# Strassen products for the FFN up projection of a four-layer decoder trunk, with the FFN in two chunks

## The chip, the cores and the metric

The kernel runs on one core of one Trainium2 chip. The metric is the device time of one execution in microseconds (us). A core has five engines, each with a queue of its own that it works through in order: TensorE (PE in the profile; its weight loads are PEld), VectorE (DVE), ScalarE (ACT), GpSimd (POOL) and SyncE (SP), which here only issues transfers. Transfers between HBM and SBUF can be issued by SP, ACT and POOL.

## The reference, cut to what matters

One sequence of 512 tokens, width 1024, passes four blocks: a short-convolution mixer, a convolutional FFN, forgetting attention with 16 heads, and a second FFN.

```
xn = rmsnorm(x, g)
up = xn @ w_up                      # 1024 -> 2 x 2816
a, g = split(up, 2)
a = causal_dwconv(a, conv_w)        # 3 taps along the sequence
x = x + (silu(a) * g) @ w_down      # 2816 -> 1024
```

All inputs are float32. The kernel works feature-major: a tile is 128 features by 512 tokens.

## The kernel before, in words

Every float32 operand of a matrix product is split into a high part (rounded to the type fp32r by an ACT copy) and a low part (the remainder, a DVE subtraction). A product of two operands is three fp32r products: high by high, high by low, low by high. `mac` (lines 124 to 132) issues these three for each half of 256 tokens, so six matmuls for one 128x128 block of weights.

Weights come in tiles of 128 columns by up to 1024 elements. `weights` (line 114) issues the load on SP (line 119) into one of three raw buffers, and `parts` (lines 110, 111) splits it in pieces of 512. `gemm` (line 134) runs over the k tiles of one output tile; `gemm2` runs two output tiles together and holds back the last k tile of both, so that the newest input is asked for late.

The FFN (line 306) has 22 up tiles. For each, `gemm` makes `pa` (the convolved half) and `pg` (the gate), 8 k tiles each, hence 96 matmuls. DVE multiplies `pa` by the norm's `r` (line 316); `conv` is one ACT scaling (line 241) and two DVE instructions (lines 242, 244); ACT applies silu (line 192); DVE scales the gate (line 322), POOL multiplies (line 323), and ACT and DVE split the product (lines 162, 163). When all 22 results stand in SBUF, `project` (line 253) makes 8 output tiles with 22 k tiles each and adds them to the residual `x` (line 271). With `spill` it also writes the new `x` tile to a DRAM tensor `xsp` (line 277), and with `spilled` it reads the old one from there (line 250). Only the first FFN spills, and only the attention reads back.

The projection of the mixer (`a_out`) feeds the first FFN, that of the attention (`b_out`) the second. Their `norm.add` calls split each new `x` tile, scaled by the norm's gain, into the operands of the next products (lines 168, 169) and sum its square (lines 222, 224).

A scheduling layer builds each engine's queue from this program; it may move an instruction past others of its engine. What stands in a queue is issued in that order, and an instruction that waits holds back all that stands behind it.

## Time and profile before

| what | value |
|---|---|
| median of three runs | 1233.29 us (1231.23 to 1235.27) |
| the profiled execution | 1233.1 us, span in the trace 1231.3 us |
| PE busy / its weight loads | 1216.5 us (99%) / 1189.0 us |
| DVE / ACT / POOL busy | 678.6 us (55%) / 537.4 us (44%) / 203.1 us (16%) |
| HBM traffic | 100 GB/s over the span |
| granted TensorE clock, mean | 0.996 |

The page gives each engine's busy time and its share of the span. Matmuls overlap in the array, so a busy PE is read together with the distance between the starts of two matmuls. Other views list groups of equal instructions, single instructions in order of time (with the idle time before one and what ended it), stretches of time, and transfers.

### The profile page before, as it was taken

The page shows a single profiled execution, that of the slowest core. Times are in us where ns is not written, and L with a number is a line of the kernel's source. Part 1 is how long each engine was busy: PE and PEld are TensorE (multiplying, and loading weights), DVE is VectorE, ACT ScalarE, POOL GpSimd, SP SyncE. Part 2 cuts the span into 40 slices and gives each one's busy share as a digit, 9 for nine tenths or more (in the row PEclk, how much of TensorE's full clock was granted, in tenths as well). Part 3 has the DMA queues.
Part 4 walks back from the last instruction along what each step waited for, and adds up shares of the span by engine and source line. Part 5 has one row for each costly group of instructions (what it writes and reads, how often), then busy time and mean ns, then how long its engine had stood idle before and what let it go on. Part 6 is the DMA issues. An engine that isn't in the chain of part 4 may idle for free.

```text
span 1231.3 us, 24568 instructions
## 1 busy us (share of the span) xinstructions
PE 1216.5 (99%) x10425; PEld 1189.0 (97%) x10425; DVE 678.6 (55%) x1163; ACT 537.4 (44%) x973; POOL 203.1 (16%) x181
## 2 busy tenths in 40 slices
PE   9999999999999999999999899999999999999998
PEld 8999999999999999999998788889999999999998
DVE  6755556555555533344646787876565555553222
ACT  5433345334333433333556767775543334342221
POOL 0100021111111100000123435442111111110000
PEclk9999999999999999999999999999999999999999
DMA  6233233333333344342342212124233233233341
GB/s 215 87 103 101 88 104 92 97 104 93 97 104 91 93 130 125 121 140 87 95 139 79 84 52 86 53 87 129 86 104 101 89 103 101 89 99 104 116 119 45
DMA packets 39374, 124.14 MB, mean 101 GB/s; under 512 B 4384, under 2 KB 4896, under 8 KB 39264
## 3 DMA queue, kind: packets, MB, share of 16 engines
q1 hardware_dynamic: 38048, 120.41, 31.8%
q10 hardware_dynamic: 1152, 1.97, 0.5%
...
q0 software_dynamic: 64, 0.20, 0.0%
HBM read 118.33 MB, written 4.23 MB: 100 GB/s over the span
## 4 chain that ended last, share of the span: by engine, by line
PE 90%; ACT 4%; DVE 3%; POOL 2%; issue 1%; DMA 0%; SPq 0%; DVEq 0%; POOLq 0%; ACTq 0%
PE st L131 18%; PE st L130 17%; PE st L132 17%; PE mm L130 11%; PE mm L132 11%; PE mm L131 11%; ACT s L189 1%; PE st L620 1%; PE at L658 1%; PE st L649 1%; POOL m L667 1%; DVE s L624 1%; DVE wlo L111 1%; ACT g L189 1%; ACT g L162 1%
## 5 line engine op out<-in xcount | busy, mean ns | idle before, releaser
L130 PE MATMUL st<-g,whi 128*128 128x256 f32 x1686 | 465.5, 276 | 0.0
L131 PE MATMUL st<-g,whi 128*128 128x256 f32 x1686 | 465.4, 276 | 0.0
L132 PE MATMUL st<-g,wlo 128*128 128x256 f32 x1686 | 465.4, 276 | 0.0
L110 ACT CAST whi<-wraw 128x512 fp32r<-128x512 f32 (+1 forms) x394 | 240.4, 611 | 473.6 <-PE st L131 291.9
L111 DVE TENSOR_TENSOR wlo<-wraw,whi 128x512 fp32r<-128x512 f32 (+1 forms) x394 | 283.6, 720 | 222.9 <-ACT whi L110 218.3
L130 PE MATMUL mm<-g,whi 128*128 128x256 f32 x1242 | 346.2, 279 | 0.0
L131 PE MATMUL mm<-g,whi 128*128 128x256 f32 x1242 | 343.5, 277 | 0.0
L132 PE MATMUL mm<-g,wlo 128*128 128x256 f32 x1242 | 343.5, 277 | 0.0
L130 PEld LDWEIGHTS st<-g,whi 128*128 128x128 f32 x1686 | 316.6, 188 | 0.1
L131 PEld LDWEIGHTS st<-g,whi 128*128 128x128 f32 x1686 | 316.5, 188 | 0.1
L132 PEld LDWEIGHTS st<-g,wlo 128*128 128x128 f32 x1686 | 316.5, 188 | 0.0
L130 PEld LDWEIGHTS mm<-g,whi 128*128 128x128 f32 x1242 | 233.5, 188 | 1.8
L131 PEld LDWEIGHTS mm<-g,whi 128*128 128x128 f32 x1242 | 233.4, 188 | 1.3
L132 PEld LDWEIGHTS mm<-g,wlo 128*128 128x128 f32 x1242 | 233.2, 188 | 0.1
L323 POOL TENSOR_TENSOR m<-m,m 128x512 f32<-128x512 f32 x44 | 69.1, 1573 | 408.3 <-DVE m L322 370.9
L162 ACT CAST g<-m 128x512 fp32r<-128x512 f32 x66 | 40.8, 619 | 90.4 <-POOL m L323 66.8
L163 DVE TENSOR_TENSOR g<-m,g 128x512 fp32r<-128x512 f32 x51 | 36.8, 722 | 67.3 <-ACT g L162 66.7
L224 POOL TENSOR_TENSOR m<-m,m 128x512 f32<-128x512 f32 x21 | 27.9, 1330 | 175.5 <-ACT m L222 153.6
L640 POOL TENSOR_SCALAR s<-s,sm 128x128 f32<-128x128 f32 (+3 forms) x64 | 41.4, 660 | 75.5 <-DVE sm L637 69.2
L189 ACT ACTIVATE s<-s,bb 128x128 f32<-128x128 f32 (+3 forms) x64 | 35.4, 555 | 22.9 <-DVE bb L633 22.8
L241 ACT ACTIVATE m<-m,pr 128x512 f32<-128x512 f32 x52 | 37.7, 725 | 15.9 <-DVE m L316 13.0
L242 DVE SCALAR_TENSOR_TENSOR m<-m,pr,m 128x511 f32<-128x511 f32 x52 | 39.0, 750 | 9.5 <-ACT m L241 9.5
...
## 6 DMA issues: line engine op xcount, KB each, us to landing
wraw<-up SPq DMA_DIRECT2D x88, 512.0 KB, 3.5
...
wraw<-a_in SPq DMA_DIRECT2D x21, 512.0 KB, 3.6
wraw<-down SPq DMA_DIRECT2D x16, 512.0 KB, 3.5
wraw<-wqg SPq DMA_DIRECT2D x16, 512.0 KB, 3.6
wraw<-a_out SPq DMA_DIRECT2D x8, 512.0 KB, 3.5
ld<-xsp SPq DMA_DIRECT2D x16, 256.0 KB, 2.8
wraw<-wv SPq DMA_DIRECT2D x8, 512.0 KB, 3.6
```

Of the source, the lines that this page charges most:

```text
L110: nc.scalar.copy(out=hi[:, :n], in_=raw)
L111: nc.vector.tensor_tensor(out=lo[:, :n], in0=raw, in1=hi[:, :n].bitcast(F32), op=ALU.subtract)
L130: nc.tensor.matmul(ps[:, f], lhsT=lh[0], rhs=rh[0][:, f], start=go, stop=False, skip_group_check=True)
L131: nc.tensor.matmul(ps[:, f], lhsT=lh[0], rhs=rh[1][:, f], start=False, stop=False, skip_group_check=True)
L132: nc.tensor.matmul(ps[:, f], lhsT=lh[1], rhs=rh[0][:, f], start=False, stop=end, skip_group_check=True)
L162: nc.scalar.copy(out=hi, in_=src)
L163: (eng or nc.vector).tensor_tensor(out=lo, in0=src, in1=hi.bitcast(F32), op=ALU.subtract)
L189: chain["exp"] = ordered(nc.scalar.activation(**kw), chain["set"])
L241: nc.scalar.activation(out=y, in_=src, func=AF.Copy, scale=pr[:, col + 2:col + 3])
L242: nc.vector.scalar_tensor_tensor(out=y[:, 1:T], in0=src[:, 0:T - 1], scalar=pr[:, col + 1:col + 2], in1=y[:, 1:T], op0=ALU.mult, op1=ALU.add)
L323: nc.gpsimd.tensor_tensor(out=g, in0=g, in1=y, op=ALU.mult)
L640: nc.gpsimd.tensor_scalar(out=s, in0=s, scalar1=sm[:, e:e + 1], scalar2=1.0, op0=ALU.mult, op1=ALU.mult)
```

## The change

The up products of one tile are a product of a 2x2 block matrix of weights (convolved half and gate, by even and odd k tiles) with a 2x2 block matrix of inputs (even and odd k tiles, by the two halves of 256 tokens). Strassen's scheme makes them with seven block products for eight: 7 x 4 k pairs x 3 = 84 matmuls of 256 columns for 96. It needs sums and differences of the weight blocks, of the input blocks, and of the products.

- Weights: a new class `Up` loads two tiles of 1024 columns (`raw[0]`, `raw[1]`) on SP. `begin` adds HBM data onto `raw[1]` by an accumulating transfer that POOL issues (line 361), splits `raw[0]` (operands `cd`, lines 373 and 374), makes one difference on POOL (line 365), splits it (ACT line 368, POOL line 369), and then adds HBM data onto `raw[0]` by a second accumulating transfer (line 370). `end` splits both sums (`eb`, `fg`). Tile j+2 is loaded and tile j+1 begun while tile j is multiplied.
- Inputs: `NormS` makes the seven combinations for each pair of `x` tiles.
- Products: seven accumulations in three PSUM banks (lines 395 to 397); ACT copies three halves out (405, 406, 417); DVE combines them into one tile `ag` (lines 424 to 426). Both POOL multiplications (461, 462) follow silu.
- Chunks: after 11 up tiles `project` runs with 11 k tiles, then again after the other 11. So `x` is read from and written to `xsp` for each chunk, and the mixer's and the attention's projections spill each tile as well.
- Weight tiles of 1024 columns are split in one piece, and most pools are replaced by one pool of 18 tiles of 1024 columns (`wide`; names beginning with `w`).

```diff
-    def project(src, hs, nk, norm, last=False, spilled=False, spill=False, pss=()):
+    def project(src, hs, norm, last=False, spilled=False, spill=False, pss=(), k0=0, minus=False):
...
+                if minus:
+                    nc.vector.tensor_tensor(out=x[m][:, f], in0=old[:, f], in1=ps[:, f], op=ALU.subtract)
...
-        project(a_out, bu, KT, nxt)
+        project(a_out, bu, nxt, spill=True)
+
+    class Up:
+        def __init__(self, w):
+            self.raw = [W(), W()]
+            self.w = w
+            nc.sync.dma_start(out=self.raw[0], in_=w[:, 0:2 * T])
+            nc.sync.dma_start(out=self.raw[1], in_=w[:, 3 * T:5 * T])
+
+        def begin(self):
+            r0, r1 = self.raw
+            nc.gpsimd.dma_start(out=r1, in_=self.w[:, 0:2 * T], accum_op=ALU.add)
+            self.cd = W(F32R), W(F32R)
+            self.split(r0, self.cd)
+            a = M()
+            nc.gpsimd.tensor_tensor(out=a, in0=r0[:, 0:T], in1=r0[:, T:2 * T], op=ALU.subtract)
+            w = W(F32R)
+            self.a = w[:, 0:T], w[:, T:2 * T]
+            nc.scalar.copy(out=self.a[0], in_=a)
+            nc.gpsimd.tensor_tensor(out=self.a[1], in0=a, in1=self.a[0].bitcast(F32), op=ALU.subtract)
+            nc.gpsimd.dma_start(out=r0, in_=self.w[:, 2 * T:4 * T], accum_op=ALU.add)
...
+            ks = range(KT // 2)
+            for some in ((ks[:-1], ks[-1:]) if first else (ks,)):
+                for n in ("3", "4", "1", "5", "2") if first else ("3", "4"):
+                    for p in some:
+                        go(n, p)
+            self.s = M()
+            nc.scalar.copy(out=self.s[:, l], in_=b43[:, r])
+            nc.scalar.copy(out=self.s[:, r], in_=b43[:, l])
...
+            nc.vector.tensor_tensor(out=ag[:, HT:HT + T], in0=self.s, in1=self.b52, op=ALU.add)
+            nc.vector.tensor_tensor(out=two(t), in0=two(self.b43), in1=b1, op=ALU.add)
+            nc.vector.tensor_tensor(out=two(ag)[:, 0:4:3], in0=two(t), in1=two(self.b52), op=ALU.subtract)
...
         for j in range(JT):
+            pair = pairs.pop(j)
+            load(j + 2)
+            begin(j + 1)
+            pair.products(norm.xs, j == 0)
...
+            if j + 1 < JT:
+                pairs[j + 1].end()
+            ag = pair.results()
             a = M()
-            nc.vector.tensor_tensor(out=a, in0=pa, in1=r, op=ALU.mult)
+            nc.vector.tensor_tensor(out=a, in0=ag[:, 0:T], in1=r, op=ALU.mult)
             y = conv(a, col + 3 * j)
             act_silu(out=y, in_=y, func=AF.Silu)
...
+            nc.gpsimd.tensor_tensor(out=y, in0=y, in1=r, op=ALU.mult)
+            nc.gpsimd.tensor_tensor(out=y, in0=y, in1=ag[:, T:2 * T], op=ALU.mult)
+            us.append(split(y))
+            if j + 1 in cuts[1:]:
...
+                project(down, us, nxt if end else None, last and end, spilled=True, spill=spill or not end, k0=cuts[c - 1],
+                        minus=True)
+                us = []
```

In SP's queue at the end of the mixer's projection, before: eight loads of `a_out` weights follow each other (the last two are shown), and the loads of the first up tiles follow them.

```order
L119 DMA wraw_2146<-a_out 128x1024
L119 DMA wraw_2213<-a_out 128x1024
L119 DMA wraw_2280<-up 128x1024
L119 DMA wraw_2333<-up 128x1024
L119 DMA wraw_2429<-up 128x1024
```

In SP's queue in the mixer's projection of the changed program, from the first `a_out` load on (`xsp<-g` writes a finished `x` tile to DRAM, `ld<-xsp` reads one back):

```order
L122 DMA w_1654<-a_out 128x1024
L122 DMA w_1703<-a_out 128x1024
L320 DMA xsp<-g_83 128x512
L320 DMA xsp<-g_84 128x512
L122 DMA w_1796<-a_out 128x1024
L290 DMA ld_3889<-xsp 128x512
L290 DMA ld_3894<-xsp 128x512
L320 DMA xsp<-g_85 128x512
L122 DMA w_1858<-a_out 128x1024
L290 DMA ld_3978<-xsp 128x512
L320 DMA xsp<-g_86 128x512
L122 DMA w_1939<-a_out 128x1024
```

From the third output tile on, the load of a tile's weights has moved behind the write of the tile before it.

In DVE's queue, one up tile of the middle of an FFN before (`wlo` are low parts of weights, `m_3147` and `m_3213` are the tile's two results, `g_3217` a low part of its product):

```order
L316 TENSOR_TENSOR m_3147<-st_3088,r_2405 128x512
L111 TENSOR_TENSOR wlo_3252<-wraw_3221,whi_3251 128x512
L242 SCALAR_TENSOR_TENSOR m_3149<-m_3147,pr,m_3149 128x511
L244 SCALAR_TENSOR_TENSOR m_3149<-m_3147,pr,m_3149 128x510
L111 TENSOR_TENSOR wlo_3290<-wraw_3287,whi_3289 128x512
L322 TENSOR_TENSOR m_3213<-st_3154,r_2405 128x512
L111 TENSOR_TENSOR wlo_3318<-wraw_3287,whi_3317 128x512
L163 TENSOR_TENSOR g_3217<-m_3213,g_3216 128x512
```

In DVE's queue, one up tile of the middle of an FFN in the changed program: call the tile whose products have just ended t (banks `mm_2948`, `st_2950`); `w_2800` and `w_2801` are the two sums of tile t+1, `w_2933` is the first raw tile of t+2, `m_2922` the result of t-1.

```order
L425 TENSOR_TENSOR m_3049<-mm_2948,m_2990 128x512
L374 TENSOR_TENSOR w_3041<-w_2800,w_3040 128x1024
L166 TENSOR_TENSOR g_2930<-m_2922,g_2929 128x512
L374 TENSOR_TENSOR w_3043<-w_2801,w_3042 128x1024
L424 TENSOR_TENSOR w_3048<-m_2975,st_2950 128x512
L426 TENSOR_TENSOR w_3048<-m_3049,st_2950 128x2x256
L458 TENSOR_TENSOR m_3053<-w_3048,r_2366 128x512
L374 TENSOR_TENSOR w_3072<-w_2933,w_3071 128x1024
L282 SCALAR_TENSOR_TENSOR m_3055<-m_3053,pr,m_3055 128x511
L284 SCALAR_TENSOR_TENSOR m_3055<-m_3053,pr,m_3055 128x510
```

The low parts of tile t+1's two sums have come to stand ahead of tile t's remaining results (L424 to L458), and the low part of tile t+2's first raw tile behind them.

In ACT's queue, one up tile before (`whi` are high parts of weights):

```order
L110 CAST whi_3251<-wraw_3221 128x512
L241 ACTIVATE m_3149<-m_3147,pr 128x512
L110 CAST whi_3289<-wraw_3287 128x512
L192 ACTIVATE m_3149<-m_3149 128x512
L110 CAST whi_3317<-wraw_3287 128x512
L162 CAST g_3216<-m_3213 128x512
```

In ACT's queue, one up tile in the changed program (`m_3053`, `m_3055` belong to tile t, `m_3075`, `w_2933` and `w_2934` to t+2, `st_3081` and `st_3082` to t+1):

```order
L373 CAST w_3071<-w_2933 128x1024
L281 ACTIVATE m_3055<-m_3053,pr 128x512
L368 CAST w_3077<-m_3075 128x512
L405 COPY m_3108<-st_3081 128x256
L406 COPY m_3108<-st_3081 128x256
L417 COPY m_3123<-st_3082 128x256
L195 ACTIVATE m_3055<-m_3055 128x512
L373 CAST w_3173<-w_2933 128x1024
L165 CAST g_3062<-m_3055 128x512
L373 CAST w_3175<-w_2934 128x1024
```

The high part of tile t+2's weight difference (L368) stands behind the conv scaling of tile t (L281). POOL's queue keeps the order of `begin`: L365, L369, L370 of a tile, then L361 of the next, then L461 and L462.

## Rows read from the trace of the kernel before

**Rows 1.** The page's busy time, share of span and instructions, by engine.

```profile
PE 1216.5 (99%) x10425; PEld 1189.0 (97%) x10425; DVE 678.6 (55%) x1163; ACT 537.4 (44%) x973; POOL 203.1 (16%) x181
```

**Rows 2.** Stretches: us; busy PE, PEld, DVE, ACT, POOL; granted clock, DMA share, GB/s.

```profile
151.00:184.30 33.30, 33.30 (x296) 33.30 (x295) 19.07 (x27) 16.43 (x28) 7.96 (x6) 1.00 0.35 109
184.30:424.80 240.50, 240.50 (x2122) 240.41 (x2121) 137.37 (x204) 99.89 (x162) 34.41 (x22) 1.00 0.32 97
424.80:543.80 119.00, 119.00 (x1052) 119.00 (x1051) 41.07 (x64) 36.98 (x63) 9.25 (x7) 1.00 0.41 121
543.80:837.90 294.10, 285.28 (x2274) 259.94 (x2274) 201.16 (x457) 185.73 (x398) 95.74 (x104) 0.98 0.28 86
837.90:868.10 30.20, 30.20 (x269) 30.20 (x268) 19.40 (x28) 15.91 (x27) 8.28 (x6) 1.00 0.47 149
```

**Rows 3.** Timeline of one up tile: start, us, engine, line, instruction, idle before.

```profile
331.34 0.28 PE L132 MATMUL st<-g,wlo 128*128 128x256 f32 x1
...
331.65 0.69 DVE L316 TENSOR_TENSOR m<-st,r 128x512 f32<-128x512 f32 x1 [1.02 <-PE st L132]
...
332.26 0.68 DVE L111 TENSOR_TENSOR wlo<-wraw,whi 128x512 fp32r<-128x512 f32 x1
...
333.14 0.75 DVE L242 SCALAR_TENSOR_TENSOR m<-m,pr,m 128x511 f32<-128x511 f32 x1 [0.20 <-ACT m L241]
...
333.92 0.75 DVE L244 SCALAR_TENSOR_TENSOR m<-m,pr,m 128x510 f32<-128x510 f32 x1
...
342.53 0.69 DVE L316 TENSOR_TENSOR m<-mm,r 128x512 f32<-128x512 f32 x1 [1.02 <-PE mm L132]
```

**Rows 4.** Groups by shape: count, busy us, mean ns of one, idle before.

```profile
L111 DVE TENSOR_TENSOR wlo<-wraw,whi 128x512 fp32r<-128x512 f32 x28 | 19.4, 693 | 46.7 <-ACT whi L110 46.7
L111 DVE TENSOR_TENSOR wlo<-wraw,whi 128x384 fp32r<-128x384 f32 x15 | 8.3, 553 | 15.1 <-ACT whi L110 15.1
...
L110 ACT CAST whi<-wraw 128x512 fp32r<-128x512 f32 x28 | 17.4, 623 | 44.5 <-PE st L131 28.4 <-PE mm L131 11.3 <-ACT m L222 4.7
L110 ACT CAST whi<-wraw 128x384 fp32r<-128x384 f32 x15 | 7.7, 514 | 26.5 <-PE st L131 17.4 <-PE mm L131 9.2
...
L241 ACT ACTIVATE m<-m,pr 128x512 f32<-128x512 f32 x19 | 13.8, 725 | 4.1 <-DVE m L316 4.1
L192 ACT ACTIVATE m<-m 128x512 f32<-128x512 f32 x19 | 11.9, 626 | 0.0
```

**Rows 5.** Groups of POOL's multiplications and differences.

```profile
L323 POOL TENSOR_TENSOR m<-m,m 128x512 f32<-128x512 f32 x44 | 69.1, 1573 | 408.3 <-DVE m L322 370.9 <-ACT m L192 37.4
L163 POOL TENSOR_TENSOR g<-m,g 128x512 fp32r<-128x512 f32 x15 | 20.0, 1335 | 7.0 <-ACT g L162 7.0
```

**Rows 6.** Timeline of POOL's transfer issue at the start.

```profile
1.25 0.73 POOL L787 DMA_DIRECT2D cs<-cst  x1 [0.81 <-POOLq L870]
```

**Rows 7.** Transfers: count, KB each, median us from issue to landing.

```profile
wraw<-a_out SPq DMA_DIRECT2D x8, 512.0 KB, 3.5
...
ld<-xsp SPq DMA_DIRECT2D x16, 256.0 KB, 2.8
...
cs<-cst POOLq DMA_DIRECT2D x1, 192.0 KB, 3.7
```

**Rows 8.** Timelines of POOL and DVE in the mixer, where they overlap.

```profile
105.87 1.29 POOL L298 TENSOR_TENSOR m<-m,r 128x512 f32<-128x512 f32 x1 [15.01 <-DVE m L244]
...
106.01 1.70 DVE L111 TENSOR_TENSOR wlo<-wraw,whi 128x512 fp32r<-128x512 f32 x1 [0.28 <-ACT whi L110]
```

**Rows 9.** Timeline of SP's queue in the first FFN's projection.

```profile
439.81 0.33 SPq L277 DMA_DIRECT2D xsp<-g  x1
440.27 0.34 SPq L119 DMA_DIRECT2D wraw<-down  x1
```

**Rows 10.** Stretches of the attention around a wait of PE.

```profile
704.20:706.50 2.30, 0.37 (x2) 0.17 (x1) 0.27 (x1) 1.44 (x3) 1.57 (x2) 0.99 0.56 217
706.50:713.30 6.80, 5.35 (x26) 4.04 (x27) 5.15 (x20) 2.70 (x10) 1.29 (x4) 0.50 0.00 1
```

More of the change, by code (lines that the diff above doesn't have):

```diff
@@ L27 @@
 KT = D // P
+HT = T // 2
 H = 16
@@ L80, in M, with W @@
         return new(misc, "m", [P, T], dtype)
+    def W(dtype=F32):
+        return new(wide, "w", [P, 2 * T], dtype)
     turn = [0]
@@ L103, in trunk, with weights @@
     ident = cs[:, C_ID:C_ID + P]
+    npr = const.tile([P, 48], F32, tag="npr", name="npr")
     def parts(raw, n):
-        hi = new(wsp, "whi", [P, T], F32R)
-        lo = new(wsp, "wlo", [P, T], F32R)
-        nc.scalar.copy(out=hi[:, :n], in_=raw)
-        nc.vector.tensor_tensor(out=lo[:, :n], in0=raw, in1=hi[:, :n].bitcast(F32), op=ALU.subtract)
+        hi, lo = W(F32R), W(F32R)
+        nc.scalar.copy(out=hi[:, :n], in_=raw[:, :n])
+        nc.vector.tensor_tensor(out=lo[:, :n], in0=raw[:, :n], in1=hi[:, :n].bitcast(F32), op=ALU.subtract)
         return [(hi[:, c:c + P], lo[:, c:c + P]) for c in range(0, n, P)]
-    def weights(src, nk=KT):
-        cuts = [0, 8] if nk == 8 else [0, 8, 15, 22]
-        for c0, c1 in zip(cuts[:-1], cuts[1:]):
-            raw = new(wraw, "wraw", [P, 1024], F32)
-            nc.sync.dma_start(out=raw[:, :(c1 - c0) * P], in_=src[:, c0 * P:c1 * P])
-            for c in range(0, c1 - c0, 4):
-                n = min(4, c1 - c0 - c) * P
-                yield from parts(raw[:, c * P:c * P + n], n)
+    def weights(src, k0, k1):
+        for c0 in range(k0, k1, 8):
+            n = (min(k1, c0 + 8) - c0) * P
+            raw = W()
+            nc.sync.dma_start(out=raw[:, :n], in_=src[:, c0 * P:c0 * P + n])
+            yield from parts(raw, n)
     def mac(ps, lh, rh, first, last):
@@ L146, in gemm2 @@
             late = []
-            for k, w in enumerate(weights(src)):
-                if k < KT - hold:
+            for k, w in enumerate(weights(src, k0, k0 + nk)):
+                if k < nk - hold:
                     mac(ps, w, xs[k], k == 0, False)
@@ L509, in attention @@
         ys = []
-        for _ in range(3):
-            yy = G(F32R)
+        y2 = W(F32R)
+        for yy in (y2[:, 0:T], y2[:, T:2 * T], G(F32R)):
             nc.vector.memset(yy.bitcast(F32), 0.0)
@@ L756, in attention @@
         kept.append(ps2)
-        for k in range(KT):
-            x[k] = None
-        project(b_out, og, KT, nxt_norm, spilled=True, pss=kept)
+        project(b_out, og, nxt_norm, spilled=True, spill=True, pss=kept)
     use_exp_ln()
```

159 lines of the change are left out of this document (113 added, 46 removed).

## The prediction

> **What bounds the kernel now.** I read the busy times of the page first: PE has work in 1216.5 us of a span of 1231.3 us, DVE in 55% of it, ACT in 44%, POOL in 16% [rows 1]. Then the stretches: in the mixer's projection, the 22 up tiles of the first FFN and its projection, PE is busy all the time at full clock; only the attention leaves it 8.8 us idle (294.10 less 285.28) [rows 2]. Then the timeline of one up tile: its first result is scaled at 331.65, the next tile's at 342.53, so a tile takes 10.88 us, and 96 matmuls in it start every 113.3 ns [rows 3]. So matmuls set the time, and what others do counts only where PE waits for it. My sum is made against the profiled execution, 1233.1 us (1.8 of it outside the span, which I leave as they are); the median of the runs shown, 1233.29, is 0.2 above.
>
> **What is removed.** Twelve of 96 matmuls in each of 44 tiles: 528 x 0.1133 = 59.8 us, and a tile's floor falls to 84 x 0.1133 = 9.52 us. This is gained only if everything else per tile fits into 9.52 us.
>
> **What is added to each up tile, by busy sums.** An element of a DVE subtraction costs (693 - 553)/128 ns, so 1024 columns take 0.69 + 4 x 0.14 = 1.25 us; an ACT copy 0.62 + 4 x 0.11 = 1.06 us [rows 4]. On DVE, 512-column instructions start 0.61 apart and the two conv steps 0.78 [rows 3]: three wide subtractions at 1.17 apart, five narrow ones at 0.61, two conv steps: 3.5 + 3.05 + 1.56 = 8.1 us. ACT: three wide copies 3.2, two of 512 1.2, conv scaling 0.73, silu 0.63, three copies of 256 columns (estimated at 0.4, by the same slope) 1.2, together 7.0 us. POOL: four instructions of 1.3 to 1.6 us [rows 5] and two transfer issues of 0.73 [rows 6], 6.7 to 7.9 us. All are under 9.52, so sums alone would call the change hidden. They do not ask who waits for whom.
>
> **The loop through five queues.** Follow the changed queues. On DVE, the low parts of tile t+1's two sums stand ahead of tile t's last results (L424 to L458). The sums come from accumulating transfers; the one onto `raw[0]` can be issued only after the previous user's steps. For tile t+2 that is, from the end of L458 of tile t: ACT scales (L281, 0.73 [rows 4]) and only then copies the difference (L368, 0.62); POOL waits for this copy (L369, 1.3 [rows 5]) and stands ahead of its own transfer issue L370; the transfer takes X from issue to landing; ACT copies the sum (L373, 1.06); DVE subtracts it (L374, 1.25), does L166 (0.61), the second sum (1.17), L424, L426 (0.61 and, as each waits for the one before it, 0.7) and L458 of tile t+1 (0.7). That closes a loop of one tile: 0.73 + 0.62 + 1.3 + X + 1.06 + 1.25 + 0.61 + 1.17 + 0.61 + 0.7 + 0.7 = 8.75 + X. I add 0.4 for POOL's wait for DVE: in the mixer a DVE subtraction that began 0.14 us after a POOL multiplication took 1.70 us for 0.68 [rows 8], so the two exclude each other, and L369 becomes ready while the conv steps run. Between no wait and both conv steps this is 0 to 1.5; the POOL row of 1573 ns, against 1335 without a DVE step at its start [rows 5], puts it near the lower end.
>
> X is in no row: the trace has no accumulating transfer. From below: an SP load of 512 KB, 3.5 [rows 7], plus the longer issue (0.73 for 0.33 [rows 6, 9]) is 3.9. A smaller value I exclude, since it must move at least what the plain load moves. From above: POOL's one transfer, 192 KB in 3.7; scaled to 512 KB by 0.7 us for 256 KB (3.5 less 2.8) it is 4.6, and reading the old contents of the tile too may cost the whole 512 KB again, 1.4, so 6.0 [rows 7]. I take 4.6, that of the nearest row. (The Trainium skill, DMA: Bandwidth & Descriptors, section Anatomy of one DMA — SWDGE (gpsimd) path, gives 2.0 us plus bytes over 436 GB/s. That is 3.2 us for 512 KB and would give 1457 where I give 1507; by it the 192 KB would have taken 2.4, and the row has 3.7, in the crowded start, so the trace does not support it here.)
>
> So a tile takes 8.75 + 0.4 + 4.6 = 13.7 us for 10.88, and PE idles 4 us of it. I count 18 of the 22 tiles of each FFN: the sums of the three behind the first chunk are issued while PE projects, and behind the last tile nothing is fetched, so these four cost about what they did. 18 x 2.8 = 50 us for each FFN.
>
> **Ends of the FFN.** At the start PE waits three times. The last `x` tile goes through the residual (0.7), ACT's scaling (0.7), a DVE step (0.75), five ACT instructions (2.9) and the copy of the weights (1.06): 6.1. Then the weights' difference has to wait for DVE's subtractions to let POOL go (1.9), L365 1.3 and L368 0.6: 3.8. Then the first sum: 1.3 + 4.6 + 1.06 less the 34 matmuls that PE has meanwhile, 3.9: 3.1. Together 13. Behind tile 11 the weights of the projection are split on ACT behind the tile's conv scaling, and PE has no next tile's products to run: the way from the last product to L458 of that tile, 8.6 in the loop above, plus 0.73 and 1.06, so 10.4; with the first low part 11. Before, these ends were covered (PE is busy 240.50 of 240.50 us [rows 2]). Each FFN: 50 + 13 + 11 = 74; both 148 us.
>
> **The spills ahead of the FFNs.** In the mixer's projection SP's queue puts the load for output tile m+1 behind the write of tile m. SP works in order: in the first FFN's projection the load follows the write by 0.46 us [rows 9]. So each load starts when the product before it is finished, and PE waits: last matmul to residual 0.31, residual 0.69 [rows 3], 0.05, write to load 0.46, load 3.5 [rows 7], copy 1.1, and, after three matmuls that need no low part (0.34), the subtraction 1.25: 7.0 us. Output tiles 3 to 8 do this: 6 x 7.0 = 42 us. The cover that goes is 33.30 us in which PE never waited [rows 2]. At the attention's end three outputs are made early, five wait 7.0, and the first of them waits for three residuals and their input sums as well (about 6): 41 us. Bounds for both: 0, if the loads were there before (the queue excludes it), to 9 per wait. In the attention's first products, all loads of V weights stand behind the last write of the FFN: 0.31 + 0.69 + four other issues at 0.46 + 3.5 + 1.1 less what the sum of squares needs anyway: about 7 and up to 14, I take 10. Extra reads and writes of `x` cost PE nothing else: the projection's 7.5 us per output cover them.
>
> **The clock.** After PE had been busy 0.37 of 2.30 us the granted clock fell from full (2.4 GHz) to half (1.2 GHz) for 6.80 us, with PE busy in 5.35 of them [rows 10]; that cost up to 2.7 us of work. Twelve of my waits (six, five and one at the attention's start) are longer than that: 12 x 2.7 = 32 us, between 0 and 50. In up tiles the waits are shorter and PE has slack against the loop, so a lower clock would not show.
>
> **Sum.** 1233.1 + 148 + 42 + 41 + 10 + 32 = 1506, say 1507 us.
>
> **Rivals.**
> A. The sum above. Its own range: X from 3.9 to 6.0 is -25 to +50 (36 tiles), POOL's wait -14 to +40, spill waits +-15, clock -32 to +18: 1440 to 1590.
> B. The sums come early (the transfer or POOL's step is covered), and DVE and POOL then exclude each other: DVE's steps with both inputs in SBUF are 3.5 + 0.61 x 2 + 1.56 = 6.3 us, POOL holds 4 x 1.15 (1.70 - 0.68 + 0.14 [rows 8]) = 4.6, so 10.9 and with handovers 11.4 per tile. For: the trace shows the exclusion. Against: X has to fall to 2.3. Price: 36 x 0.5 + 48 + 42 + 41 + 10 + 32 = 191, so 1424. (The Trainium skill, SBUF — State Buffer, section Who interferes with whom, has it as a lock held for the whole instruction; the 1.70 us agree.)
> C. An accumulating transfer is far slower than a load, X = 8. For: no row shows one. 36 x (17.1 - 10.88) = 224, so 1233 + 224 + 48 + 125 = 1630.
> D. The busy sums decide: every queue fits under the 9.52 us and the queues do not close a loop, because transfers are issued a tile further ahead than I read. Place: the up tiles; price -60; it decides as soon as the loop spans two tiles. With the early loads that it needs the spill waits go too: 1173, plus 2 x 13 for the starts, 1199: faster. Against: L369, L370 and the order on DVE, and the exclusion, by which DVE and POOL need 10.9.
>
> **How the numbers follow.** A 0.72, B 0.13, C 0.11, D 0.03, 0.01 for other ways to about the old time. A measurement tells 0.3% (3.7 us) from no change. A, B and C are slower: 0.96; D is faster: 0.03; same 0.01. The time is A's, 1507. The range runs from 1405 (B with slightly fewer waits) to 1610 (A's upper end, part of C); D and most of C stay outside.
>
> **What would show it.** An up tile's period in DVE's timeline, from one L458 to the next: 13.7 us (B: 11.4; D: 9.5). The `raw[0]` accumulation's time to landing: 4.6. ACT's wide copy of the sum waiting for that transfer, not for PE. In the mixer's projection a wait of PE of about 6 us ahead of each of the output tiles 3 to 8, with SP's load following the write. Half clock in these stretches. I am wrong if the up tiles start under 11 us apart, or if PE runs through the mixer's projection.

## The result, and the profile after

The changed kernel takes 1572.37 us (median of four runs, 1571.35 to 1573.83) against 1233.82 us (four runs, 1231.23 to 1235.27). The ratio is 1.2748, with a 95% interval of 1.2723 to 1.2772. The forecast was slower, 1507 us, between 1405 and 1610.

The first part of the page of the profiled execution (1572.9 us, span 1570.7):

```profile
PE 1292.5 (82%) x9897; PEld 1233.1 (79%) x9897; DVE 826.4 (53%) x1163; ACT 618.2 (39%) x1036; POOL 452.1 (29%) x401
```

No engine is full any more: PE, in use for 99% of the span before [rows 1], stands still for 278 us of the span, and no other engine passes 53%. Such a page calls for the view of stretches next. These are the stretches of the changed kernel (busy us and instructions of PE, PEld, DVE, ACT, POOL; granted clock; share and GB/s of transfers): the mixer's projection with the first wait of the FFN, the first FFN in four pieces (first tile; ten tiles; the first chunk's projection; the rest), the attention, its projection, the second FFN:

```profile
150.30:246.80 96.50, 49.81 (x291) 46.66 (x290) 30.56 (x41) 24.91 (x39) 10.14 (x8) 0.74 0.23 77
246.80:275.50 28.70, 21.96 (x144) 20.69 (x145) 14.39 (x15) 10.15 (x15) 10.49 (x10) 0.81 0.80 195
275.50:420.40 144.90, 110.07 (x784) 104.91 (x783) 89.96 (x100) 61.88 (x100) 71.67 (x60) 0.89 0.65 146
420.40:497.20 76.80, 73.37 (x627) 73.08 (x628) 28.91 (x35) 19.65 (x27) 6.48 (x5) 0.95 0.52 156
497.20:707.90 210.70, 173.69 (x1357) 168.14 (x1355) 117.21 (x134) 82.74 (x132) 76.88 (x64) 0.94 0.51 127
707.90:1009.80 301.90, 285.31 (x2238) 258.29 (x2238) 190.08 (x420) 180.68 (x361) 93.88 (x103) 0.97 0.26 84
1009.80:1106.70 96.90, 50.65 (x300) 47.65 (x300) 32.19 (x42) 24.60 (x39) 11.14 (x9) 0.72 0.23 80
1106.70:1570.70 464.00, 379.94 (x2906) 367.65 (x2906) 244.45 (x275) 163.00 (x256) 156.77 (x132) 0.91 0.56 140
```

Against the same stretches of before [rows 2] (33.3, 359.5, 294.1, 30.2, and 363.2 up to the end), with the forecast's terms sorted into them (the first wait of each FFN, 6.1 us, counted with the projection ahead of it; 2.7 us of half clock for each spill wait):

| stretch | before | after | more | forecast more |
|---|---|---|---|---|
| mixer's projection | 33.3 | 96.5 | 63.2 | 42 + 16 + 6 = 64 |
| first FFN | 359.5 | 461.1 | 101.6 | 74 - 6 = 68 |
| attention | 294.1 | 301.9 | 7.8 | 10 + 3 = 13 |
| its projection | 30.2 | 96.9 | 66.7 | 41 + 14 + 6 = 61 |
| second FFN | 363.2 | 464.0 | 100.8 | 74 - 6 = 68 |

Four stretches, of two kinds, account for 332 of the 340 us: the projections and the FFNs.

**An up tile.** The timeline of one up tile of the first FFN, from one scaling L458 to the next (start, us, engine, line, idle time before and what ended it; instructions beside the chain left out; the last row from DVE's own timeline):

```profile
319.56 0.69 DVE L458 TENSOR_TENSOR m<-w,r 128x512 f32<-128x512 f32 x1
...
320.28 0.72 ACT L281 ACTIVATE m<-m,pr 128x512 f32<-128x512 f32 x1 [2.53 <-DVE m L458]
320.91 0.60 ACT L368 CAST w<-m 128x512 fp32r<-128x512 f32 x1
...
321.59 1.60 POOL L369 TENSOR_TENSOR w<-m,w 128x512 fp32r<-128x512 f32 x1 [7.42 <-ACT w L368]
...
323.14 0.87 POOL L370 DMA_DIRECT2D w<-up  x1
...
328.67 1.06 ACT L373 CAST w<-w 128x1024 fp32r<-128x1024 f32 x1 [4.20 <-DMA w<-up]
...
329.76 1.23 DVE L374 TENSOR_TENSOR w<-w,w 128x1024 fp32r<-128x1024 f32 x1 [2.19 <-ACT w L373]
330.90 0.68 DVE L166 TENSOR_TENSOR g<-m,g 128x512 fp32r<-128x512 f32 x1
331.50 1.22 DVE L374 TENSOR_TENSOR w<-w,w 128x1024 fp32r<-128x1024 f32 x1
332.64 0.68 DVE L424 TENSOR_TENSOR w<-m,st 128x512 f32<-128x512 f32 x1
333.23 0.68 DVE L426 TENSOR_TENSOR w<-m,st 128x512 f32<-128x512 f32 x1
333.95 0.69 DVE L458 TENSOR_TENSOR m<-w,r 128x512 f32<-128x512 f32 x1
```

This is the forecast's loop, instruction by instruction: each starts within 0.1 us of the end of the one before, and L373 waits for the transfer, not for PE. Closed chains of this kind are read by adding: if the pieces add up to the period with no pause left, nothing outside the chain sets it. The median of 30 such tiles is 14.6 us (10.88 before [rows 3]); from the start of L370 to that of L373 it is 5.70.

**The mixer's projection.** The timeline around the wait behind one output tile:

```profile
180.47 0.32 SPq L320 DMA_DIRECT2D xsp<-g  x1
180.48 0.72 ACT L255 ACTIVATE w<-g,pr 128x512 f32<-128x512 f32 x1 [8.88 <-DVE g L314]
180.85 0.42 SPq L122 DMA_DIRECT2D w<-a_out  x1
...
184.05 0.40 ACT L271 CAST g<-m 128x256 fp32r<-128x256 f32 x1
184.46 1.05 ACT L113 CAST w<-w 128x1024 fp32r<-128x1024 f32 x1
185.56 0.58 PE L131 MATMUL st<-g,w 128*128 128x256 f32 x1 [5.84 <-ACT w L113]
```

PE waits 5.84 us here, 6.1 to 6.7 from matmul to matmul, six times, and SP's load follows the write of `x` by 0.38 us, as forecast. But two things end at the same moment. The load lands 3.6 us after its issue, at 184.44; and ACT's copy L113 has no idle time before it, since it follows directly on ACT's six instructions for the new `x` tile (180.48 to 184.45). Behind every other tile the norm has two instructions only, and there the copy waits for the load alone (2.9 to 3.3 us, three times). In the attention's projection the load ends the copy's wait all five times. What would be left if the load came earlier, this trace does not tell; so this is the first experiment.

### The profile page after: what moved, and what is told of

Its sections match the earlier page's. It is cut to its first block, busy times and chain, and to the rows that moved or that the text cites. A ratio compares the mean times of both kernels' runs of the same rounds, so it can differ in the third digit from the quotient of the medians.

```text
span 1570.7 us, 24067 instructions
## 1 busy us (share of the span) xinstructions
PE 1292.5 (82%) x9897; PEld 1233.1 (79%) x9897; DVE 826.4 (53%) x1163; ACT 618.2 (39%) x1036; POOL 452.1 (29%) x401
## 3 DMA queue, kind: packets, MB, share of 16 engines
q0 software_dynamic: 12736, 46.34, 16.8%
## 4 chain that ended last, share of the span: by engine, by line
PE 44%; issue 18%; POOL 15%; DVE 10%; DMA 7%; ACT 6%; SPq 0%; POOLq 0%; DVEq 0%; ACTq 0%
PE st L133 7%; PE st L131 7%; PE st L132 7%; PE mm L133 6%; PE mm L131 6%; PE mm L132 6%; DMA w<-up 4%; POOL m L461 3%; POOL m L462 3%; POOL w L369 3%; POOL m L365 2%; DVE w L374 2%; POOL w L361 1%; DVE w L114 1%; POOL w L370 1%
## 5 line engine op out<-in xcount | busy, mean ns | idle before, releaser
L395 PE MATMUL st<-g,w 128*128 128x256 f32 x880 | 268.0, 306 | 68.4 <-ACT w L373 38.0
L131 PE MATMUL st<-g,w 128*128 128x256 f32 x846 | 246.8, 292 | 68.7 <-ACT w L113 68.7
L397 PE MATMUL st<-g,w 128*128 128x256 f32 x880 | 266.4, 304 | 25.7 <-DVE w L374 25.7
L131 PE MATMUL mm<-g,w 128*128 128x256 f32 x834 | 239.5, 287 | 35.9 <-ACT w L113 32.9
L396 PE MATMUL st<-g,w 128*128 128x256 f32 x880 | 262.3, 299 | 0.0
L133 PE MATMUL st<-g,w 128*128 128x256 f32 x846 | 246.3, 291 | 8.5 <-DVE w L114 8.5
L395 PEld LDWEIGHTS st<-g,w 128*128 128x128 f32 x880 | 185.2, 211 | 77.2 <-ACT w L373 42.3
L374 DVE TENSOR_TENSOR w<-w,w 128x1024 fp32r<-128x1024 f32 x132 | 165.5, 1261 | 152.1 <-ACT w L373 152.1
L132 PE MATMUL st<-g,w 128*128 128x256 f32 x846 | 244.5, 289 | 0.0
L133 PE MATMUL mm<-g,w 128*128 128x256 f32 x834 | 236.5, 284 | 2.7 <-DVE w L114 2.7
L132 PE MATMUL mm<-g,w 128*128 128x256 f32 x834 | 235.9, 283 | 0.0
L131 PEld LDWEIGHTS st<-g,w 128*128 128x128 f32 x846 | 170.6, 202 | 71.3 <-ACT w L113 71.2
L397 PEld LDWEIGHTS st<-g,w 128*128 128x128 f32 x880 | 185.2, 211 | 32.1 <-DVE w L374 32.1
L114 DVE TENSOR_TENSOR w<-w,w 128x384 fp32r<-128x384 f32 (+1 forms) x125 | 137.8, 1109 | 131.3 <-ACT w L113 127.1
L373 ACT CAST w<-w 128x1024 fp32r<-128x1024 f32 x132 | 133.9, 1048 | 184.0 <-DMA w<-up 182.6
L131 PEld LDWEIGHTS mm<-g,w 128*128 128x128 f32 x834 | 161.9, 194 | 39.0 <-ACT w L113 33.8
L396 PEld LDWEIGHTS st<-g,w 128*128 128x128 f32 x880 | 185.6, 211 | 0.0
L133 PEld LDWEIGHTS st<-g,w 128*128 128x128 f32 x846 | 169.7, 201 | 12.0 <-DVE w L114 11.9
L113 ACT CAST w<-w 128x384 fp32r<-128x384 f32 (+1 forms) x125 | 112.1, 911 | 149.1 <-DMA w<-down 111.5
L132 PEld LDWEIGHTS st<-g,w 128*128 128x128 f32 x846 | 170.4, 201 | 0.0
L369 POOL TENSOR_TENSOR w<-m,w 128x512 fp32r<-128x512 f32 x44 | 71.1, 1616 | 342.0 <-ACT w L368 236.2
L133 PEld LDWEIGHTS mm<-g,w 128*128 128x128 f32 x834 | 161.4, 193 | 3.9 <-DVE w L114 3.9
```

The lines of the kernel that those rows point to most:

```text
L113: nc.scalar.copy(out=hi[:, :n], in_=raw[:, :n])
L114: nc.vector.tensor_tensor(out=lo[:, :n], in0=raw[:, :n], in1=hi[:, :n].bitcast(F32), op=ALU.subtract)
L131: nc.tensor.matmul(ps[:, f], lhsT=lh[0], rhs=rh[0][:, f], start=go, stop=False, skip_group_check=True)
L132: nc.tensor.matmul(ps[:, f], lhsT=lh[0], rhs=rh[1][:, f], start=False, stop=False, skip_group_check=True)
L133: nc.tensor.matmul(ps[:, f], lhsT=lh[1], rhs=rh[0][:, f], start=False, stop=end, skip_group_check=True)
L369: nc.gpsimd.tensor_tensor(out=self.a[1], in0=a, in1=self.a[0].bitcast(F32), op=ALU.subtract)
```

## The experiments

Each kernel ran on the chip with before beside it. Where nothing else is said a time is that of one profiled execution, against 1572 of the changed kernel. "Period" is the distance between two L458.

### Is it the write of `x`, or the norm?

```diff
-                nc.sync.dma_start(out=xsp[m], in_=x[m])
+                nc.scalar.dma_start(out=xsp[m], in_=x[m])
```

> Edit: the changed kernel, but x's tiles are written out (L320) from ACT's queue instead of SP's. Theory S (the prediction's: SP's load of the next weights stands behind the write of x): the six waits of PE in the mixer's projection (6.1 to 6.7 us each, 1.0 to 1.4 behind most) and the five in the attention's projection (12.4 once, then 6.2 to 6.6) go, with their half clock: the mixer's projection from 90 to about 45 us, the other one by as much, about 1475 in all. Theory N (ACT's queue: the copy L113 of the next tile's weights stands behind the six instructions of the next norm that wait for x; behind the odd tiles it starts in the trace with no idle time before it): the waits behind odd tiles stay at 6, those behind even tiles fall from 6.3 to about 4: 11 waits lose some 15 us in all, so 1550 to 1560.

Measured: 1570.3, no change. Timelines of PE, SP and ACT in the mixer's projection, two waits behind output tiles that follow each other:

```profile
170.00 0.38 PE L131 MATMUL st<-g,w 128*128 128x256 f32 x1 [2.99 <-ACT w L113]
170.19 1.85 SPq L122 DMA_DIRECT2D w<-a_out  x4
...
184.37 1.04 ACT L113 CAST w<-w 128x1024 fp32r<-128x1024 f32 x1
185.46 0.58 PE L131 MATMUL st<-g,w 128*128 128x256 f32 x1 [5.73 <-ACT w L113]
```

The next four loads are issued at 170.2, and the copy still starts at 184.37, behind the norm. The waits alternate, short behind the tiles after which the norm has two instructions to do and long where it has six: theory N, with its numbers for this projection (3.3 and 6.0 from matmul to matmul). The first up tile comes 8.4 us earlier, but 4.4 of that are lost again in the attention's projection, where the waits are now 7.0 to 7.3 us, and 1.6 in the FFNs; N's 15 us were not won. In the mixer's projection, then, the write alone is not what costs the time. In the attention's projection this run is no test of S. Timelines of SP and ACT there:

```profile
1052.94 0.38 SPq L122 DMA_DIRECT2D w<-b_out  x1
...
1057.43 1.04 ACT L113 CAST w<-w 128x1024 fp32r<-128x1024 f32 x1 [3.65 <-DMA w<-b_out]
```

The load is as late as ever, because it still stands behind the read of `x` (L290, at 1052.53), which waits for DVE's L314; and the copy waits for the load, 1.0 to 3.7 us, all five times.

```diff
-    wide = ctx.enter_context(tc.tile_pool(name="wide", bufs=18))
+    wide = ctx.enter_context(tc.tile_pool(name="wide", bufs=14))
+    nwide = ctx.enter_context(tc.tile_pool(name="nwide", bufs=4))
...
-                self.xg = W()
+                self.xg = new(nwide, "nw", [P, 2 * T], F32)
...
-            xg, t, one = self.xg, W(), M()
+            xg, t, one = self.xg, new(nwide, "nw", [P, 2 * T], F32), M()
```

> Edit: the changed kernel, with the same 18 wide buffers cut into 14 for weights and results and 4 for the two wide tiles that NormS takes for each pair of x tiles; the writes of x stay on SP. In its order SP's loads of the projection's weights and ACT's copies of them then stand ahead of the writes and of NormS. Theory N, with the shared buffers as what put both behind NormS: PE's waits in both projections go and the clock stays at full there, 1572 - 95 = about 1475 (between 1455 and 1490). Theory S has nothing that would move the loads; by it 1572.

Measured: 1469.5. The mixer's projection in that kernel, columns as above:

```profile
150.30:185.00 34.70, 34.70 (x308) 34.61 (x306) 22.66 (x33) 17.13 (x29) 10.93 (x9) 1.00 0.44 141
```

PE is busy in 34.70 of 34.70 us at full clock, as before the change [rows 2], with the writes of `x` still on SP. So neither the spill nor Strassen's norm as work costs the 130 us of the two projections: it is that the norm's wide tiles were drawn from the same 18 buffers as the weights, in the order of the program, and so loads and copies of later weights were put behind a norm that waits for `x`. (The edit moves loads and copies together, so this run does not weigh one against the other.) The first scaling comes 66.6 us earlier and the way from the last one of the first FFN to the first one of the second is 62.5 us shorter; 13 and 16 us were given back at the breaks behind tile 11, with 14 buffers.

```diff
-    n2 = NormS("ffn0")
+    n2 = Norm("ffn0")
...
-            pair = pairs.pop(j)
-            load(j + 2)
-            begin(j + 1)
-            pair.products(norm.xs, j == 0)
+                pa = gemm(up[j, 0], norm.xs)
```

> Edit: the changed kernel without Strassen: the FFNs' up products in eight blocks with Norm as before, but in two chunks of 11 tiles, with x written out and read back as in the changed kernel. Theory S (writes of x ahead of the loads on SP cost the 11 waits): 1233 + 83 of waits + about 15 of half clock + 10 at the attention's start, 1340. Theory N: no NormS, so nothing stands ahead of the loads: 1233 + two breaks behind tile 11 and the attention's later start, 1240 to 1265.

Measured: 1268.4 and 1281.5, ratio to before 1.0338 (1.0199 to 1.0477). Theory S's 1340 is out; N's range is missed by 3 and 17 us. In the profiled run PE never waits in the projection, the FFNs and behind tile 11 (230.00 of 230.00 us from 200 to 430, where the break lies), yet a tile of the first FFN takes 11.31 us and one of the second 10.88: its matmuls start 118 ns apart for 113 at a granted clock of 1.00, from about 195 us to 915, where the second FFN's tiles begin. What that is stays open. Chunks and spills alone cost some 35 to 48 us, not the 125 that the prediction gave to waits that it ascribed to the spills.

### Does the loop through the transfer set the period?

```diff
             nc.scalar.copy(out=self.a[0], in_=a)
-            nc.gpsimd.tensor_tensor(out=self.a[1], in0=a, in1=self.a[0].bitcast(F32), op=ALU.subtract)
-            nc.gpsimd.dma_start(out=r0, in_=self.w[:, 2 * T:4 * T], accum_op=ALU.add)
+            sent = nc.gpsimd.dma_start(out=r0, in_=self.w[:, 2 * T:4 * T], accum_op=ALU.add)
+            ordered(nc.gpsimd.tensor_tensor(out=self.a[1], in0=a, in1=self.a[0].bitcast(F32), op=ALU.subtract), sent)
```

> Edit: the changed kernel, with POOL issuing the accumulating transfer onto raw[0] (L370) ahead of the low part L369, which it doesn't need. Loop theory: the way from the end of L458 to the issue is now 0.04 + 0.63 + 0.63 + 0.1 + 1.55 = 2.95 us (L281, L368, L369); then it is only DVE's L374 of the weights, 1.2 to 1.3. The period falls from 14.6 to 13.0, and with it 18 or 19 tiles of each FFN: 37 x 1.6 = 60, 1512. Rival (POOL and DVE excluding each other, or the transfers themselves, set the period): 14.6 stays, 1572.

Measured: 1559.8, period mostly 13.9: neither 13.0 nor 14.6. Timelines of DVE and POOL (in this kernel the transfer is L369 and the low part L370):

```profile
329.52 1.30 POOL L462 TENSOR_TENSOR m<-m,w 128x512 f32<-128x512 f32 x1
330.79 1.31 POOL L365 TENSOR_TENSOR m<-w 128x512 f32<-128x512 f32 x1
331.27 3.04 DVE L374 TENSOR_TENSOR w<-w,w 128x1024 fp32r<-128x1024 f32 x2 [1.03 <-ACT w L373]
...
336.14 0.69 DVE L458 TENSOR_TENSOR m<-w,r 128x512 f32<-128x512 f32 x1
336.76 1.22 DVE L374 TENSOR_TENSOR w<-w,w 128x1024 fp32r<-128x1024 f32 x1
...
338.52 0.87 POOL L369 DMA_DIRECT2D w<-up  x1 [6.43 <-DVE w L374]
```

The issue follows DVE's subtraction by 0.54 us, not at once: it starts 2.38 us after L458, for 3.58 in the changed kernel (319.56 to 323.14), so 1.2 us of the hoped 1.6 left the loop. And POOL's multiplication and difference now fall beside the two wide subtractions, which take 3.04 us for 2.36: 0.68 come back. 14.55 - 1.2 + 0.68 = 14.03, near the 13.9 measured. The loop is the right account; the gain of an earlier issue is partly paid back to the exclusion of DVE and POOL.

```diff
-            nc.gpsimd.dma_start(out=r1, in_=self.w[:, 0:2 * T], accum_op=ALU.add)
+            nc.gpsimd.dma_start(out=r1, in_=self.w[:, 0:2 * T])
...
-            nc.gpsimd.dma_start(out=r0, in_=self.w[:, 2 * T:4 * T], accum_op=ALU.add)
+            nc.gpsimd.dma_start(out=r0, in_=self.w[:, 2 * T:4 * T])
```

> Edit: the changed kernel with both transfers of POOL's queue as plain loads (the two sums of weights are left out), issued at the same places. Theory P (adding doubles the work of each packet: in the changed kernel's trace a packet of 4 KB takes 0.34 us in these transfers and 0.16 to 0.18 in SP's loads, eight of them follow each other on each DMA engine): issue to use falls from 5.7 by 8 x 0.17 = 1.35 to 4.35, the period from 14.55 to 13.2, 37 x 1.35 = 50, 1522. Theory Q (the way through POOL's queue is what is long, whatever it carries): 5.7 and 14.55 stay, 1572. The prediction's X of 4.6, scaled from POOL's plain transfer before, lies at P's value for a plain one.

Measured: 1511.7, period 12.97, and 3.84 us from issue to use for 5.70: theory P, with somewhat more effect. The queue's row on the page (packets, MB, share of 16 engines' span), of the changed kernel and then of this one:

```profile
q0 software_dynamic: 12736, 46.34, 16.8%
```

```profile
q0 software_dynamic: 12736, 46.34, 9.1%
```

The same bytes take 264 us of the 16 engines' time (16.8% of 1570.7) when they are added and 137 (9.1% of 1509.5) when they are not: nearly double, and over 88 transfers 1.4 us each. POOL's issue takes 0.87 us for 0.58. Together these are 1.7 of the 1.86 us that X loses.

```diff
-            nc.gpsimd.dma_start(out=r1, in_=self.w[:, 0:2 * T], accum_op=ALU.add)
...
-            nc.gpsimd.dma_start(out=r0, in_=self.w[:, 2 * T:4 * T], accum_op=ALU.add)
```

> Edit: the changed kernel without the two accumulating transfers (the sums of weights are left out; every copy, subtraction and product stays). The loop through the transfer is gone, so the period is what is next. Loop alone with PE behind it: 9.6 us, 37 x 4.9 = 180, 1390. Rival B of the prediction (DVE and POOL exclude each other): 10.9 to 11.4, 37 x 3.4 = 125, 1445. Theory E (the order in DVE's, ACT's and POOL's queues holds each tile's steps one behind the other, with the exclusion on top: of the 14.55 us only the 5.7 less the wait for the difference L369 of 2.3 goes): 12.5 to 13.2, 37 x 1.7 = 63, about 1510.

Measured: 1494.1, period 12.2 to 13.5, mostly 12.5: theory E. Without any transfer a second closed chain stands right behind the first. The timeline of this kernel (line numbers from L364 on are lower by one to two than in the changed kernel: L456 is the scaling, L459 and L460 the two multiplications):

```profile
309.92 0.69 DVE L456 TENSOR_TENSOR m<-w,r 128x512 f32<-128x512 f32 x1
...
310.64 0.72 ACT L281 ACTIVATE m<-m,pr 128x512 f32<-128x512 f32 x1 [2.89 <-DVE m L456]
...
311.67 0.74 DVE L282 SCALAR_TENSOR_TENSOR m<-m,pr,m 128x511 f32<-128x511 f32 x1
...
312.44 1.65 DVE L284 SCALAR_TENSOR_TENSOR m<-m,pr,m 128x510 f32<-128x510 f32 x1
...
314.19 0.63 ACT L195 ACTIVATE m<-m 128x512 f32<-128x512 f32 x1 [0.55 <-DVE m L284]
...
314.90 1.48 POOL L459 TENSOR_TENSOR m<-m,r 128x512 f32<-128x512 f32 x1 [1.35 <-ACT m L195]
...
316.46 2.15 POOL L460 TENSOR_TENSOR m<-m,w 128x512 f32<-128x512 f32 x1
...
318.64 0.62 ACT L165 CAST g<-m 128x512 fp32r<-128x512 f32 x1 [2.88 <-POOL m L460]
...
319.30 1.13 DVE L166 TENSOR_TENSOR g<-m,g 128x512 fp32r<-128x512 f32 x1 [1.83 <-ACT g L165]
...
322.38 0.69 DVE L456 TENSOR_TENSOR m<-w,r 128x512 f32<-128x512 f32 x1
```

DVE has the low part L166 of this tile ahead of the next tile's results (L422 to L424, from 320.35) and its scaling, so the way through conv, silu and POOL's two multiplications closes a loop of 12.46 us. In it L284, L459, L460 and L166 are longer where the other of the two engines works: against 0.75, 1.29, 1.29 and 0.68 alone, 0.90 + 0.19 + 0.86 + 0.45 = 2.4 us of it are exclusion. Even with sums for nothing a tile takes more than the 10.88 of before.

```diff
-            nc.gpsimd.tensor_tensor(out=y, in0=y, in1=r, op=ALU.mult)
-            nc.gpsimd.tensor_tensor(out=y, in0=y, in1=ag[:, T:2 * T], op=ALU.mult)
```

> Edit: the one above, and in addition POOL's two multiplications behind the silu (L461, L462) are left out; POOL then has L365 and L369 alone. If the exclusion of DVE and POOL sets the period without the transfers, each of the two gives back the 1.15 us that DVE lost to it: 2.3 us less than the run above per tile, for 40 tiles some 90 us. If the order of the queues alone sets it, only their own place between the silu and the low part goes, which nothing waits for in the same tile: no change against the run above, within 15 us.

Measured: 1398.1, period 9.9 to 11.2. It fell by 2.3 us a tile, as the first alternative said; but both multiplications (3.6 us) stand on the second loop, so the fall does not separate exclusion from order. The second alternative was wrong to say that nothing waits for them.

### Two loops, opened one by one

```diff
+    wide = ctx.enter_context(tc.tile_pool(name="wide", bufs=16))
+    nwide = ctx.enter_context(tc.tile_pool(name="nwide", bufs=2))
...
+            sent = nc.gpsimd.dma_start(out=r0, in_=self.w[:, 2 * T:4 * T], accum_op=ALU.add)
```

> Edit: the changed kernel with 16 shared wide buffers and 2 of NormS's own, and with the accumulating transfer ahead of L369. In the kernel with 14 and 4 the way from tile 11 to tile 14 behind the break took 138 and 139 us for 124 and 123: if the four fewer shared buffers did that, it returns to 124 here, 1469 - 29 = 1440; the transfer's earlier issue takes another 12 to 24 (it took 12 from the changed kernel, with periods of 13.9 for 14.55): 1416 to 1430. If the longer break comes from the loads' new order instead, 1445 to 1457.

Measured: 1443.6, between the two ranges. The way across the break (four distances, from the scaling of tile 11 to that of tile 15) takes 132 us in the first FFN and 128 in the second, for 124 and 123 in the changed kernel with 18 shared buffers and 138 and 139 with 14. With two of the four buffers given back, about half of the longer break is gone. That fits the buffers, but no run separates them from the loads' new order.

```diff
-            self.raw = [W(), W()]
+            self.raw = [W(), W(), W()]
...
+            nc.sync.dma_start(out=self.raw[2], in_=w[:, 2 * T:4 * T])
...
+            nc.gpsimd.dma_start(out=r2, in_=self.w[:, 0:2 * T], accum_op=ALU.add)
...
-            nc.gpsimd.dma_start(out=r0, in_=self.w[:, 2 * T:4 * T], accum_op=ALU.add)
```

> Edit: the changed kernel with 16 shared wide buffers and 2 of NormS's own, and with the first sum made in a third buffer: SP loads half of it there, POOL adds the other half, so that the transfer waits neither for L369 nor for any step of an earlier tile. Base: the run with 16 and 2 and the earlier issue (1443.6) less what that issue gave (12.6 alone), 1456. One-loop theory: the transfer's loop sets 14.55; without it the 12.5 of the run without sums are left: 37 x 2.05 = 76, 1380. Two-loop theory (in the run without sums a second loop closes: L281, L284, silu L195, POOL's L461 and L462, L165, and L166 ahead of the next tile's results on DVE, 12.47 us; POOL's two transfer issues of 0.6 to 0.9 stand in the same queue and lengthen it): 13.5 to 14.1, 1420 to 1440.

Measured: 1440.6, at the upper end of the two-loop theory, but the periods fit neither theory: mostly 12.9 to 13.0 before the break, 14.0 to 16.9 behind it. Behind the break the timelines of DVE and POOL show something new, in four tiles of the first FFN and three of the second:

```profile
536.81 1.60 POOL L463 TENSOR_TENSOR m<-m,r 128x512 f32<-128x512 f32 x1
537.19 6.97 DVE L376 TENSOR_TENSOR w<-w,w 128x1024 fp32r<-128x1024 f32 x1 [1.08 <-ACT w L375]
...
541.14 1.92 POOL L368 TENSOR_TENSOR m<-w 128x512 f32<-128x512 f32 x1
```

POOL runs four instructions one behind the other (L463, L372, L464, L368, to 543.06), and a subtraction of DVE that takes 1.22 alone ends only behind the last of them. The exclusion costs DVE 5.75 us in this tile. In the seven tiles such a subtraction takes 5.9 to 7.6 us; before the breaks none takes more than 3.0. Why POOL's work lines up so behind the break was not followed.

```diff
-            nc.gpsimd.tensor_tensor(out=y, in0=y, in1=r, op=ALU.mult)
-            nc.gpsimd.tensor_tensor(out=y, in0=y, in1=ag[:, T:2 * T], op=ALU.mult)
+            nc.vector.tensor_tensor(out=y, in0=y, in1=r, op=ALU.mult)
+            nc.vector.tensor_tensor(out=y, in0=y, in1=ag[:, T:2 * T], op=ALU.mult)
```

> Edit: 16 and 2 buffers as above, the sums as in the changed kernel, but L461 and L462 (the two multiplications behind the silu) on DVE instead of POOL. One-loop theory and two-loop theory agree that the transfer's loop stays; it loses only POOL's overlap with DVE's steps: 14.0 to 14.5 and 1440 to 1456. If it falls under 13, neither holds and POOL's load is what counts.

Measured: 1440.3, period mostly 13.6 to 14.2: the transfer's loop stays, as both theories say.

```diff
+            self.raw = [W(), W(), W()]
...
+            nc.vector.tensor_tensor(out=y, in0=y, in1=r, op=ALU.mult)
+            nc.vector.tensor_tensor(out=y, in0=y, in1=ag[:, T:2 * T], op=ALU.mult)
```

> Edit: both of the two runs above in one kernel; nothing is left out. Two-loop theory: both loops are open, and what is left is DVE's own sum (8.1 us and two multiplications of 0.68, so 9.5, with POOL's two remaining instructions excluding it for some 1.2 each at most): 10.4 to 11.5 us a tile, 1456 - 37 x 3.5 = about 1325, while each edit alone gives under 40. One-loop theory: no more than the third buffer alone gives, within 20 us.

Measured: 1369.3 and 1372.7, ratio to before 1.1112 (1.1061 to 1.1164). Each edit alone gives about 15 us against the estimated base of 1456, both together 85; the one-loop theory, by which both give at most 20 us more than the third buffer alone, is out. But two loops of nearly one length are not the whole account. The ten distances from the first scaling of a chunk to its last (us, first FFN / second FFN):

| kernel | first chunk | second chunk |
|---|---|---|
| changed kernel | 144.9 / 146.3 | 142.2 / 141.7 |
| third buffer | 131.3 / 132.5 | 142.9 / 143.2 |
| gate on DVE | 139.2 / 140.8 | 135.4 / 138.0 |
| both | 129.3 / 129.1 | 117.1 / 115.9 |

In the first chunk the third buffer alone gives 14 of the 16 to 17 us that both give: the transfer's loop set the period there, and the next bound lies close behind it. The gain beyond the sum comes from the second chunk. There the third buffer alone gives nothing, with POOL's four instructions holding DVE up, and two of the four are the multiplications that the other edit takes away. My 1325 was too low, since the period is 12.84 in the first chunk (11.2 to 13.4 mostly in the second). DVE's timeline tells why:

```profile
306.37 1.67 DVE L464 TENSOR_TENSOR m<-m,w 128x512 f32<-128x512 f32 x1
307.96 3.89 DVE L376 TENSOR_TENSOR w<-w,w 128x1024 fp32r<-128x1024 f32 x2
...
315.89 0.75 DVE L283 SCALAR_TENSOR_TENSOR m<-m,pr,m 128x511 f32<-128x511 f32 x1 [0.79 <-ACT m L282]
```

From one L283 (at 303.06) to the next there is one pause of 0.79 us in 12.84: DVE itself is the bound, with 2.5 us of stretched steps.

```diff
-            nc.gpsimd.tensor_tensor(out=a, in0=r0[:, 0:T], in1=r0[:, T:2 * T], op=ALU.subtract)
+            nc.vector.tensor_tensor(out=a, in0=r0[:, 0:T], in1=r0[:, T:2 * T], op=ALU.subtract)
...
-            nc.gpsimd.tensor_tensor(out=self.a[1], in0=a, in1=self.a[0].bitcast(F32), op=ALU.subtract)
+            nc.vector.tensor_tensor(out=self.a[1], in0=a, in1=self.a[0].bitcast(F32), op=ALU.subtract)
```

> Edit: the run with the third buffer and the gate on DVE (1371), and POOL's last two instructions per tile, L365 and L369, on DVE too; POOL then only issues the two transfers. Theory X (DVE and POOL exclude each other): in that run DVE has no pause but 0.79 us in a period of 12.84, and three of its steps are long beside POOL's two instructions (L464 1.67 for 0.68, a pair of subtractions 3.89 for 2.36), 2.5 us; DVE takes over 2 x 0.61 to 0.68 and gives back 2.5: 12.84 - 2.5 + 1.3 = 11.6 down to DVE's own 10.9 where its pause closes too; 37 x 1.2 to 1.9 in all: 1300 to 1325. Rival (the long steps are long for another reason and DVE is simply full): 12.84 + 1.3, 37 x 1.3 = 48 more, about 1420. Neither is under the 1233 before, since a tile still takes what it took before, and the starts, the breaks and the attention's end come on top.

Measured: 1325.4 (four runs, 1322.7 to 1327.6), ratio to before 1.0732 (1.0702 to 1.0763). Giving the full engine two more instructions made the kernel 45 us faster. DVE's timeline, the same steps:

```profile
304.35 0.68 DVE L464 TENSOR_TENSOR m<-m,w 128x512 f32<-128x512 f32 x1
305.58 2.36 DVE L376 TENSOR_TENSOR w<-w,w 128x1024 fp32r<-128x1024 f32 x2 [0.55 <-ACT w L375]
```

1.67 is 0.68 again and 3.89 is 2.36. Theory X holds; the period is 10.8 to 11.8 in the first chunk. (The Trainium skill, SBUF — State Buffer, section Who interferes with whom, says that a DVE instruction with two SBUF inputs contends with a GpSimd instruction that reads SBUF, and calls the shared port pair an exclusive lock; these rows agree.) This is the best version with Strassen's products that was found, and it is slower than before: its tiles take about what a tile took before the change (11.2 on the mean of a chunk for 10.88), so the matmuls that Strassen saves are not gained, and starts and breaks remain.

## Why the prediction held, point by point

- **Direction and mechanism of the up tiles: right.** The loop has the forecast's steps in the forecast's order; all but X add up to 8.9 us for 9.15.
- **X: the term that was mis-sized.** Taken 4.6 from POOL's one plain transfer; measured 5.70, inside its bounds of 3.9 to 6.0 and near the upper one, that of a transfer which also reads the old contents. The plain load on the same queue takes 3.84. (The Trainium skill's formula, DMA: Bandwidth & Descriptors, section Anatomy of one DMA — SWDGE (gpsimd) path, gives 3.2; both measurements are above it.)
- **Eighteen tiles of each FFN: half right.** I let the three tiles behind the break cost what they did. They take 18.60, 14.92 and 13.92 us, 15 more than three old ones (13 in the second FFN): only one tile's sum is ready after the projection, since SP issues the next loads at 491.45, behind the last write and read of `x`. With the writes on ACT's queue the first of these took 17.75, so the writes alone are not what holds the loads; that was not followed further.
- **The break behind tile 11: 11 us forecast; PE waits 9.3 and 11.3. The start of an FFN: 13 forecast, 6.4 + 2.5 + 2.8 + 1.3 measured.** The break's 8.6 from the last product to the scaling follows from no sum of the loop; it measured 6.8 and 8.8, so the hit is partly luck.
- **The clock in the FFNs: a term left at nothing.** I gave it no price outside the spill waits. The granted clock is 0.81 in the first tile shown, 0.89 in the ten behind it and 0.95 in the projection. Of the 34 us above forecast in the first FFN, 20 are X and the tiles behind the break (15 tiles at 14.57 for 10.88, which is 55, and the 15 above, for 50 forecast). Of the other 14, 5 are half clock at the start of its two projections, where matmuls start 213 ns apart for 113 (granted clock 0.84 from 422.8 to 440.0 and 0.67 from 639.8 to 650.0); up to 4.5 are slower matmuls in the first tile. The rest, in starts, breaks and ends, I cannot split.
- **The spills: the size right, the cause half the story.** 64 and 61 us were forecast for the two projections, 63 and 67 measured; in each, the matmuls between the waits lose 14 us to half clock, for 16 and 14 forecast. The forecast's chain did occur: each load follows the write, and each of the eleven copies that PE waits for starts within 0.25 us of its load's landing. But the write ahead of the load is not all that holds PE: in the mixer's projection, with the write elsewhere, three of six waits shrink by half, the others stay, and the time with them. ACT's copies stood behind the norm, as both drew on one pool of buffers, and the norm's ACT chain happens to be as long as write and load. The prediction had looked at SP's queue alone; ACT's showed the same order, and the pool behind both orders was not in it.
- **Rivals.** B's exclusion is real and, with DVE's own steps, became the bound once the transfer's loop was open, at 12.8 rather than 11.4 us; C's X of 8 and D's two-tile loop did not occur.
